# Channel tiles of an input projection in pairs, by seven products of quarters in place of eight

## Chip, core and metric

The kernel runs on one core of a Trainium2 chip. The metric is the device time of one execution in microseconds (us); the median of three runs is given where one number stands for a kernel. A profile is one further execution, recorded by the hardware.

## The reference

One layer of a hybrid model for 128 context tokens and 512 latent tokens, width 1024. The input projection `u = h @ w_in` gives all inputs of two head groups:

```python
h = _rms(x, norm_pre_w) * (1 + scale) + shift            # scale, shift, gate from c @ w_mod
u = h @ w_in                                             # 1024 -> 6176 columns
z, xbc, dt_raw, q, k, v, g = jnp.split(u, ...)
xbc = silu(_dwconv(xbc, conv_w, conv_b))                 # 3 taps along the tokens
xs, Bm, Cm = jnp.split(xbc, ...)
y_s, sf, sb = _bidir(Cm, Bm * dt, ..., xs, ...)          # chunked scans, both directions
y_s = _rms((y_s + D * xs) * silu(z), ssd_norm_w)
y_r, rf, rb = _bidir(rope(q), rope(k), ..., v, ...)      # retention, per-head decay
y_r = groupnorm(y_r) * ret_norm_w * silu(g)
out = concat([y_s, y_r]) @ w_out
y = x + gate * _rms(out, norm_post_w)
```

Outputs are `y` for both token sets and the final scan states of the context tokens. Everything is fp32.

## The kernel before

Every large product is made in three terms: each operand is split into a high part in the fp32r type and the fp32r remainder, and high x high, high x low and low x high are added up in PSUM. Activations are split once (`hh`, `hl`, 8 row tiles of 128 x 640 tokens); weights come as pieces of 256 KB (`raw`), are cast on ScalarE (`whi`, line 174) and subtracted on VectorE (`wlo`, line 175, drawn with the helper's line 131). `feed` (182) issues loads and splits some pieces ahead of their use, `take` (190) hands them out.

A start phase, written out by hand in `START` (44), normalises and modulates the activations while a first product (`gemm0`) already runs. Then the work goes by four head groups. `gemm_r` (447) makes v and g of a group by `gemm_wide` (432: five PSUM banks of 512 columns, one for each token tile, filled side by side) and q and k by `gemm_tok` (417: one token tile after the other, evicted by `ev_qk`, 384, which applies the rotation). `gemm_s` (505) makes the four channel tiles B, C and two of xs, `gemm_z` (514) two gate tiles of the group before, all by `gemm_ch` (463): channels on the partitions, 640 tokens as two halves of 320 columns, 8 row tiles x 3 terms x 2 halves = 48 matmuls a tile. `ev_conv` (478) copies the halves to `u` and does the convolution and SiLU, `ev_z` (494) the gate.

Beside these products run small steps of the scan (`s_steps`, 761) and of retention (`r_steps`, 614). They are given due times in slots: `slot` (201) is called between matmuls, feeds the weights and emits the steps that are due; an iteration over a group has 66 slots (20 in v/g, 10 in q/k, 12 in z, 24 in the channel tiles). `job` (207) spreads a list of steps over slots, lines 926 to 938. The framework then orders each engine's instructions by their place in the program, taking a later one where an earlier one is not expected to be ready; each engine's queue is in order on the chip.

Retention and scan results go to DRAM (`mixd`) and are loaded back (`load_mix`, 1003), scaled and split for the output product: `gemm_wide` three times and, for the last 512 columns, `gemm_out` (1020) in blocks of 256 columns. `ev_last` (1076) and `out_row` (1064) normalise, gate and store.

## Time and profile before

| | |
|---|---|
| median of 3 runs | 606.78 us (606.14 to 609.61) |
| profiled execution | 606.02 us, of which the span from first to last instruction is 604.0 us |
| granted TensorE clock | 0.993 of full speed over the span |
| busy share of TensorE, VectorE, ScalarE, GpSimd | 96%, 69%, 56%, 5% |
| DMA | 87.44 MB, mean 145 GB/s |

The busy share is an average over stages. TensorE's matmuls overlap and their ends are modelled, so its share isn't read as peak use; the distance from the start of one matmul to the start of the next is the better price. VectorE and ScalarE work through their queues in order.

### The profile page before, as it was taken

What the parts mean: (1) busy time and instruction counts of PE and PEld (TensorE: products, weight loads), DVE (VectorE), ACT (ScalarE), POOL (GpSimd) and SP (SyncE); (2) the same over time, 40 slices, a digit from 0 to 9 for tenths busy, and PEclk for the clock granted to TensorE, in tenths of its full rate; (3) what the DMA queues carried; (4) which work ended last, traced back from release to release, by engine and by line L of the source; (5) the groups of instructions that cost most, each with busy time, mean ns of one, the idle gap of its engine ahead of it and who ended that gap; (6) DMA issues with size and microseconds to landing.
All of it is one profiled execution on the core that took longest, in us unless ns stands there. A gap on an engine that the chain in (4) does not pass through costs nothing.

```text
span 604.0 us, 10966 instructions
## 1 busy us (share of the span) xinstructions
PE 582.3 (96%) x3833; PEld 521.5 (86%) x3833; DVE 418.1 (69%) x942; ACT 337.4 (56%) x934; POOL 31.3 (5%) x112
## 2 busy tenths in 40 slices
PE   5899998999999999999999999999999999999995
PEld 3577998978999998889999888999999777788895
DVE  3657498855698866668897746798867866743665
ACT  5436255665667764465766646566755857262421
POOL 1000001200000010000011000000110000000010
PEclk9899999999999999999999999999999999999998
DMA  8694231553335633232554223354537777384033
GB/s 348 229 362 161 63 105 48 162 146 109 99 97 159 185 91 86 80 122 70 189 172 112 76 69 105 102 163 131 160 96 223 209 266 221 116 272 120 18 109 135
DMA packets 47638, 87.44 MB, mean 145 GB/s; under 512 B 5792, under 2 KB 18656, under 8 KB 46048
## 3 DMA queue, kind: packets, MB, share of 16 engines
q1 hardware_dynamic: 47296, 86.57, 45.2%
q8 instruction: 30, 0.49, 0.3%
q14 instruction: 24, 0.20, 0.1%
q10 hardware_dynamic: 288, 0.18, 0.1%
HBM read 75.03 MB, written 9.60 MB: 140 GB/s over the span
## 4 chain that ended last, share of the span: by engine, by line
PE 65%; DVE 13%; ACT 9%; DMA 6%; issue 5%; POOL 2%; SPq 0%; POOLq 0%; DVEq 0%; ACTq 0%
PE gw L123 24%; PE gc L123 11%; PE gt L123 9%; PE acc L123 5%; PE go L123 4%; DMA cf<-cumd 3%; PE ss L123 2%; PE mod L123 2%; DVE wlo L131 2%; DVE SC L128 2%; PE sfb L123 1%; PE ry L123 1%; POOL sm L131 1%; DVE yc L128 1%; ACT jk L733 1%
## 5 line engine op out<-in xcount | busy, mean ns | idle before, releaser
L131 DVE TENSOR_TENSOR wlo<-raw,whi 128x512 fp32r<-128x512 f32 (+1 forms) x120 | 82.2, 690 | 49.2 <-ACT whi L174 48.3
L174 ACT CAST whi<-raw 128x512 fp32r<-128x512 f32 (+1 forms) x120 | 73.6, 619 | 76.3 <-PE gw L123 46.1
L123 PE MATMUL gc<-hh,whi 128*128 128x320 f32 x384 | 96.7, 331 | 0.0
L123 PE MATMUL gc<-hl,whi 128*128 128x320 f32 x384 | 88.3, 310 | 0.0
L123 PE MATMUL gc<-hh,wlo 128*128 128x320 f32 x384 | 87.6, 309 | 0.0
L123 PEld LDWEIGHTS gc<-hh,whi 128*128 128x128 f32 x384 | 63.9, 189 | 1.1
L123 PEld LDWEIGHTS gc<-hl,whi 128*128 128x128 f32 x384 | 64.3, 188 | 0.1
L123 PEld LDWEIGHTS gc<-hh,wlo 128*128 128x128 f32 x384 | 64.1, 188 | 0.0
L123 PE MATMUL gw<-whi,hh 128*128 128x512 f32 x120 | 50.6, 421 | 0.8 <-ACT u L484 0.8
L123 PE MATMUL gw<-whi,hl 128*128 128x512 f32 x120 | 47.0, 392 | 0.0
L123 PE MATMUL gw<-wlo,hh 128*128 128x512 f32 x120 | 46.8, 390 | 0.0
L123 PE MATMUL gt<-whi,hh 128*128 128x256 f32 (+1 forms) x160 | 46.3, 289 | 0.0
L123 PE MATMUL gt<-wlo,hh 128*128 128x256 f32 (+1 forms) x160 | 45.7, 286 | 0.0
L123 PE MATMUL gt<-whi,hl 128*128 128x256 f32 (+1 forms) x160 | 45.7, 286 | 0.0
L862 ACT ACTIVATE m<-gu,dt 128x128 f32<-128x128 f32 x80 | 31.3, 391 | 16.5 <-DVE gu L131 14.6
L834 ACT ACTIVATE cf<-cf,dmc 128x128 f32<-128x128 f32 x80 | 26.5, 393 | 18.4 <-DMA cf<-cumd 18.4
L131 DVE TENSOR_TENSOR m<-m,cf 128x512 f32<-128x512 f32 x40 | 27.5, 689 | 8.8 <-ACT cf L863 8.2
L123 PE MATMUL gw<-whi,mrh 128*128 128x512 f32 x80 | 32.3, 404 | 0.0
L123 PE MATMUL gw<-wlo,mrh 128*128 128x512 f32 x80 | 31.2, 391 | 0.0
L123 PEld LDWEIGHTS gt<-whi,hh 128*128 128x128 f32 x160 | 30.5, 190 | 0.7 <-issue 0.5
L863 ACT ACTIVATE cf<-gu,dt 128x128 f32<-128x128 f32 x80 | 31.0, 387 | 0.0
L123 PE MATMUL gw<-whi,mrl 128*128 128x512 f32 x80 | 30.9, 391 | 0.0
(232 smaller groups left out, 1327.8 us busy)
## 6 DMA issues: line engine op xcount, KB each, us to landing
raw<-ws SPq DMA_DIRECT2D x116, 256.0 KB, 2.8
cf<-cumd SPq DMA_DIRECT2D x20, 512.0 KB, 4.2
wm<-wm SPq DMA_DIRECT2D x8, 1024.0 KB, 8.2
mraw<-mixd SPq DMA_DIRECT2D x16, 320.0 KB, 3.4
ef<-ecumd SPq DMA_DIRECT2D x32, 128.0 KB, 3.3
wg<-wg SPq DMA_DIRECT2D x4, 1024.0 KB, 5.9
x<-x SPq DMA_DIRECT2D x5, 512.0 KB, 7.3
mixd<-rmix SPq DMA_DIRECT2D x20, 128.0 KB, 2.7
```

What stands on the lines that cost most here:

```text
L123: r = pe.matmul(out, lhsT=a, rhs=b, start=start, stop=stop)
L128: eng.scalar_tensor_tensor(out=out, in0=in0, scalar=s, in1=in1, op0=op0, op1=op1)
L131: return eng.tensor_tensor(out=out, in0=a, in1=b, op=op)
L174: act.copy(hi, raw)
L733: act.activation(jk, yc[:, h], AF.Square, scale=P ** -0.5, accum_out=sm[:, 2 + h:3 + h])
L834: act.activation(cf[:, e, 1, q], cf[:, e, 1, q], AF.Identity, bias=dmc[:, c, h:h + 1])
L862: act.activation(m[:, e, q], gu[:, 0], AF.Copy, scale=dt[:, c, h:h + 1])
L863: act.activation(cf[:, e, 1, q], gu[:, 1], AF.Copy, scale=dt[:, c, 16 + h:17 + h])
```

## The change

**Pairs.** Two channel tiles are made together by `gemm_pair`: the 1024 rows of the weights fall into two halves, the two tiles are two column halves, and the tokens fall into two halves of 322 columns (640 tokens and two zero columns behind the context tokens and two at the end, `TW`, `HW`, `off`). A 2 x 2 product of blocks is then made with seven block products in place of eight, after Winograd's form of Strassen's method. Sums of activation halves are made once (`sums`, into `sh`, `sl`); sums of weight blocks are made per pair: two of the seven pieces by a load followed by a load that adds onto it, issued by GpSimd, and two by VectorE from pieces that are there. Three PSUM banks hold the seven products in turn, and VectorE and ScalarE take them out between the products.

**Work area.** To make room for `sh` and `sl`, the scan's buffers (`sw`) and retention's (`rw`) are allocated and released in turn in one area, so the two no longer overlap in time; the due times change with that.

**Beside these.** q and k are made by `gemm_wide` too, with all five token tiles side by side; the first product takes its weights from the same stream; there are six `raw` buffers and five of `whi`, `wlo` in place of four and seven, and pieces are split four ahead; the scan's skip term is added in its own steps; the last output product uses 512 columns, and its weights are split into the place of `hh`, `hl`; the retention half of the output product's input is loaded into the memory of the right-hand area that `rp` and `tp` (`sh`, `sl`) had.

The core of the diff:

```diff
-START: ... H7:0123 G6:34 G6:012 H7:4 F2 G7:012 G7:34
+START: ... H7:0123 T0 G6:34 G6:012 T1 H7:4 F2 G7:012 T2 G7:34        # T: sums
@@ plan
+    def pair(a, b):
+        lo, hi = list(range(4)), list(range(4, 8))
+        a11, a12, a21, a22 = (("w_in", k, [(c, c + P)]) for c in (a, b) for k in (lo, hi))
+        load(*a11)
+        want.append(("sum", (-1, 2)))
+        load(*a11, a21)
+        load(*a21, a22)
+        load(*a12)
+        want.append(("sum", (-4, -1)))
+        load(*a22)
@@ load, split, feed
+            if i:
+                pool.dma_start(out=out, in_=src, accum_op=ALU.add)
+            else:
+                sp.dma_start(out=out, in_=src)
...
+    def split(n):
+        raw = pieces[n]
+        for m in (n + 1, n + 4):
+            if m < len(want) and want[m][0] == "sum" and n - m == min(want[m][1]):
+                x, y = (pieces[m + d] for d in want[m][1])
+                tt(pieces[m], x, y, ALU.add)
...
+        act.copy(hi, raw)
+        tt(lo, raw, hi.bitcast(F32), ALU.subtract)
...
+        while state["ld"] < min(len(want), state["sp"] + 6, state["use"] + 10):
+            load(state["ld"])
+            state["ld"] += 1
+        while state["sp"] < min(first, state["ld"], state["use"] + 4):
+            split(state["sp"])
+            state["sp"] += 1
@@ activations
+    def sums(k):
+        a, b, c, d = (rows[k + i][:, h * HW:(h + 1) * HW] for i in (0, 4) for h in range(2))
+        tt(d, b, d, ALU.subtract)
+        tt(b, a, b, ALU.subtract)
+        tt(a, d, a, ALU.subtract)
+        tt(c, c, a, ALU.add)
+        for i in range(2):
+            r = rows.pop(k + 4 * i)
+            q = slice(2 * i, 2 * i + 2)
+            hi, lo = (x[:, k, q].rearrange("p q t -> p (q t)") for x in (sh, sl))
+            act.copy(hi, r)
+            tt(lo, r, hi.bitcast(F32), ALU.subtract)
@@ q and k
-        gemm_tok(288 if p == 0 else 256, lambda t, ps: ev_qk(p, t, ps))
+        gemm_wide(hh, hl, lambda t, ps: ev_qk(p, t, ps), off, *((288, 1) if p == 0 else (256, 2)))
@@ channel tiles: gemm_ch, ev_conv and ev_z go
+    def gemm_pair():
+        ua, ub = (us[(turn["u"] + e) % 4] for e in range(2))
+        turn["u"] += 2
+        a0, a1, b0, b1 = (u[:, 1 + h * HW:1 + (h + 1) * HW] for u in (ua, ub) for h in range(2))
+        s1 = sp_.tile([P, HW], F32, tag="s1", name="s1", bufs=2)
+        X, Y, Z = (pg.tile([P, 512], F32, tag="g", name="gc")[:, 0:HW] for _ in range(3))
...
+        steps = [
+            (X, half(0, 0), True, lambda: act.copy(s1, X)),
+            (Y, sm(0), True, lambda: tt(b0, Y, s1, ALU.add)),
+            (Z, sm(3), True, None),
+            (Y, sm(1), False, lambda: (tt(b1, Y, s1, ALU.add), tt(b1, Z, b1, ALU.subtract))),
+            (X, half(0, 4), False, lambda: act.copy(a0, X)),
+            (Y, half(1, 4), False, lambda: tt(a1, Y, s1, ALU.add)),
+            (Z, sm(2), False, lambda: tt(b0, Z, b0, ALU.subtract)),
+        ]
+        for n, (ps, of, first, then) in enumerate(steps):
+            wh, wl = take()
+            for i in range(4):
+                xh, xl = of(i)
+                mm(ps, wh[:, i], xh, first and i == 0, False, again=True)
+                mm(ps, wh[:, i], xl, False, False, again=True)
+                mm(ps, wl[:, i], xh, False, i == 3, big=True, again=True)
+                if i == 3 and then:
+                    then()
+                if i == 3 or (i == 1 and n < 5):
+                    slot()
+        return ua, ub
@@ due times
-    job(dt_steps(), 11, 24.5)
-    job(r_steps(0), 10, 33)
+    job(dt_steps(), 10.5, 22)
+    job(r_steps(0), 12, 33)
...
-        s_job(g - 1, n + 2.5, n + 43.5, n + 51.75)
+        a, b = s_steps(g - 1)
+        job(a, n + 1, n + 36)
         gemm_r(g)
-        job(r_steps(g), n + 31.25, n + 67.25)
+        job(r_steps(g), n + 37, n + 65.5)
         gemm_z(g - 1)
+        job(b, n + 42.5, n + 43.5)
         gemm_s(g)
@@ the scan's chunk, its skip term
+                    for e in range(2):
+                        y = S[g]["xs"][e][:, off(c):off(c) + P]
+                        stt(y, y, pkc(PK_D, 2 * g + e), o[:, e])
+                if 4 in cs:
+                    sw[0].release()
@@ output product
-    ldr = load_mix(1, mrh, mrl, wp, 4)
+    ldr = load_mix(1, mrh, mrl, op)
...
+            for a, n in ((0, 512),) if t < NCK - 1 else ((0, 256), (256, 256)):
```

## Rows read from the trace of the kernel before

**Rows 1.** The page: busy time and share of each engine; the chain by engine.
```profile
PE 582.3 (96%) x3833; PEld 521.5 (86%) x3833; DVE 418.1 (69%) x942; ACT 337.4 (56%) x934; POOL 31.3 (5%) x112
...
PE 65%; DVE 13%; ACT 9%; DMA 6%; issue 5%; POOL 2%; SPq 0%; POOLq 0%; DVEq 0%; ACTq 0%
```

**Rows 2.** Windows: stretch, length, busy (x) of PE, PEld, DVE, ACT, POOL; clock; DMA.
```profile
62.60:78.60 16.00, 16.00 (x122) 16.00 (x121) 7.50 (x23) 4.47 (x14) 0.27 (x6) 1.00 0.12 32
78.60:122.40 43.80, 41.27 (x291) 39.69 (x290) 37.93 (x107) 24.91 (x82) 6.55 (x19) 1.00 0.39 115
283.50:340.00 56.50, 56.10 (x409) 54.85 (x409) 47.06 (x98) 39.41 (x120) 5.32 (x19) 1.00 0.47 141
...
230.70:340.00 109.30, 108.34 (x730) 100.84 (x729) 80.47 (x173) 67.15 (x195) 5.73 (x23) 1.00 0.39 116
```

**Rows 3.** Timeline of TensorE (start, length, instruction): columns 320, 512, 256.
```profile
305.45 0.46 PE L123 MATMUL gc<-hh,whi 128*128 128x320 f32 x2
...
306.92 0.46 PE L123 MATMUL gc<-hh,wlo 128*128 128x320 f32 x2
...
470.64 0.39 PE L123 MATMUL gw<-wlo,mrh 128*128 128x512 f32 x1
470.87 0.39 PE L123 MATMUL gw<-whi,mrh 128*128 128x512 f32 x1
...
596.81 0.28 PE L123 MATMUL go<-whi,msh 128*128 128x256 f32 x1
...
596.93 0.28 PE L123 MATMUL go<-wlo,msh 128*128 128x256 f32 x1
```

**Rows 4.** Groups of VectorE by line, whole span: busy us, mean ns, idle before.
```profile
L131 DVE TENSOR_TENSOR wlo<-raw,whi 128x512 fp32r<-128x512 f32 (+1 forms) x120 | 82.2, 690 | 49.2 <-ACT whi L174 48.3
L128 DVE SCALAR_TENSOR_TENSOR zg<-zth,gc 128x320 f32<-128x320 f32 x16 | 7.1, 483 | 1.1 <-ACT zth L498 1.1
L128 DVE SCALAR_TENSOR_TENSOR xs<-u,cw,xs 128x641 f32<-128x641 f32 x16 | 14.2, 886 | 6.5 <-ACT xs L486 6.3
L128 DVE SCALAR_TENSOR_TENSOR xs<-cth,xs 128x641 f32<-128x641 f32 x8 | 6.6, 826 | 0.7 <-ACT cth L490 0.7
```

**Rows 5.** Timeline of VectorE, two independent neighbours.
```profile
306.75 0.68 DVE L131 TENSOR_TENSOR wlo<-raw,whi 128x512 fp32r<-128x512 f32 x1
307.35 0.68 DVE L131 TENSOR_TENSOR Sst<-Sst,els 128x512 f32<-128x512 f32 x1
```

**Rows 6.** VectorE's groups in 283.5 to 340.0, and (last two) in 230.7 to 283.5.
```profile
L131 DVE TENSOR_TENSOR m<-m,cf 128x512 f32<-128x512 f32 x6 | 4.1, 689 | 0.2
L131 DVE TENSOR_TENSOR cf<-cf 128x512 f32<-128x512 f32 x3 | 2.1, 685 | 0.7 <-ACT cf L834 0.7
L128 DVE SCALAR_TENSOR_TENSOR y<-xs,pk,y 128x512 f32<-128x512 f32 x2 | 1.4, 750 | 0.0
...
L131 DVE TENSOR_TENSOR ta<-gt,rope 128x256 f32<-128x256 f32 x4 | 1.7, 423 | 1.5 <-PE gt L123 1.5
L131 DVE TENSOR_TENSOR kw<-rk,rtail 128x256 f32<-128x256 f32 x2 | 0.8, 420 | 0.0
```

**Rows 7.** A window in which VectorE is densest over 20 us.
```profile
76.62:96.62 20.00, 18.72 (x135) 18.37 (x135) 19.13 (x56) 9.99 (x28) 0.17 (x3) 1.00 0.29 83
```

**Rows 8.** The output product's first matmul (timeline), and its input's load (DMA issues, 466 to 480).
```profile
468.96 2.98 ACT L1009 ACTIVATE mrh<-mraw,nrm 128x640 fp32r<-128x640 f32 x4
...
469.84 0.50 PE L123 MATMUL gw<-whi,mrh 128*128 128x512 f32 x1
...
mraw<-mixd SPq DMA_DIRECT2D x4, 320.0 KB, 3.6
```

**Rows 9.** DMA issues (KB each, median us to landing), and a GpSimd step (timeline).
```profile
raw<-ws SPq DMA_DIRECT2D x116, 256.0 KB, 2.8
cf<-cumd SPq DMA_DIRECT2D x20, 512.0 KB, 4.2
...
304.96 0.71 POOL L131 TENSOR_TENSOR sm<-sm,mhalf 128x2 f32<-128x2 f32 x1
```

More of the change, by code (lines that the diff above doesn't have):

```diff
@@ L21 @@
 T = 640
+TW = 644
+HW = 322
 NCK = 5
@@ new lines, in plan, with sources @@
+        pair(B0 + p * P, C0 + p * P)
+        pair(XS0 + p * 256, XS0 + p * 256 + P)
+    pair(Z0 + 768, Z0 + 768 + P)
+    for half, cb in ((1, 0), (1, 2), (0, 0), (0, 2)):
+        for k in range(KT):
+            load("w_out", [8 * half + k], [(cb * 256, cb * 256 + 512)])
+    return want
+def sources():
+    at, size, order = {}, 0, []
+    for kind, of in plan():
+        for m, rows, cols in of if kind == "load" else ():
+            key = (m, tuple(rows), tuple(cols))
+            if key not in at:
+                at[key] = size
+                size += len(rows) * sum(b - a for a, b in cols)
+                order.append((m, rows, cols))
+    return at, size, order
@@ L178, in body, with load @@
[L178 to L184 removed]
+    where = sources()[0]
+    state = {"ld": 0, "sp": 0, "use": 0}
+    pieces, split_of, late = {}, {}, {}
+    def load(n):
+        kind, of = want[n]
+        nk, c = (4, P) if kind == "sum" else (len(of[0][1]), sum(b - a for a, b in of[0][2]))
+        raw = pieces[n] = wp.tile([P, nk, c], F32, tag="raw", name="raw", bufs=6)
+        for i, (m, rows, cols) in enumerate(of if kind == "load" else ()):
+            a = P * where[m, tuple(rows), tuple(cols)]
+            src = io["ws"][a:a + P * nk * c].rearrange("(p x) -> p x", p=P)
+            out = raw.rearrange("p k c -> p (k c)")
+            if i:
+                pool.dma_start(out=out, in_=src, accum_op=ALU.add)
+            else:
+                sp.dma_start(out=out, in_=src)
@@ L198, in body, with take @@
+    def take():
+        feed()
+        n = state["use"]
+        state["use"] += 1
+        pieces.pop(n)
+        return split_of.pop(n)
     jobs = []
@@ L321, in h_tile @@
         ash = ash_t[kt]
[L322 removed]
+        row = h_row(kt)
         tr = bank("tr")
```

438 lines of the change are left out of this document (201 added, 237 removed).

## Prediction

> **What bounds the kernel now.** I read the page's busy shares and its chain first, then the stages by window, then inside one stage the groups by line and the order in time. The shares name TensorE: busy 96% of the span, and 65% of the chain is its matmuls [rows 1]. VectorE, at 69%, looks as if it had room. The windows say otherwise [rows 2]: an iteration over a head group (109.3 us) has a first part, 52.8 us long, where VectorE works 33.4 us, and a second part, the channel tiles (283.5 to 340.0), where it works 47.1 of 56.5 us, 83%. In the channel tiles of group 0 it is 37.9 of 43.8 us, 87%. TensorE sets the end everywhere, but in the stages that this change rewrites VectorE is close behind. That is the thing to see before costing anything: the change takes work from TensorE and gives work to VectorE, in the same stages.
>
> **TensorE's part.** Matmuls of 320 columns start 0.147 us apart (ten of them, five rows, from 305.45 to 306.92) [rows 3], so the spacing, not the 0.31 to 0.33 us that one is drawn with, is its price. A pair of tiles costs 96 of them now, 14.1 us; after, 7 products x 4 row tiles x 3 terms = 84 of 322 columns, at 0.148 us (the spacing scaled by 322/320) 12.4 us. Saved: 1.7 us a pair, 20.4 us over 12 pairs. The last output product has 240 matmuls of 256 columns at 0.12 us (28.8 us) and gets 96 of 512 at 0.23 and 48 of 256 at 0.12 [rows 3], 27.8 us: 1.0 us less. If nothing else moved, the kernel would lose 21 us.
>
> **VectorE's part, per pair.** Seven pieces of weights are split in place of four, so three more subtractions; two pieces are sums that VectorE makes itself; five half-tile evictions (322 columns, out of PSUM) replace copies of ScalarE. One subtraction is 0.69 us, one 320-column operation that reads PSUM 0.48 us [rows 4]. Independent neighbours overlap: the one at 306.75 takes 0.68 us, and the next starts 0.60 us later [rows 5]. I therefore charge 0.60 for 512 columns and 0.40 for 322: 5 x 0.60 + 5 x 0.40 = 5.0 us a pair, 60 us in all. No row shows the sum of two pieces; the subtraction has its shape and operand count, so I take that. The z pairs replace four half-tile operations by two full ones, which is even.
>
> **The channel stage of an iteration (before: 56.5 us, VectorE 47.1).** Three pairs add 15.0. The scan now ends six slots into this stage rather than thirteen, because scan and retention take turns in one area: two of the three chunks that fall here leave (two thirds of 4.1 for m and of 2.1 for cf, and about 1.8 of their smaller steps) [rows 6], minus 5.9. The skip term (1.4) [rows 6] goes into the scan's own steps, of which one chunk stays: minus 0.9. Against that, the q/k product now finishes its five token tiles together, so three of four rotations (1.2 us each: the 0.42 and the small ones behind it [rows 6], less the overlap) slide in: plus 3.5. Retention starts after the scan, not 1.25 slots before this stage's own work: plus 2.2 for its key weighting (0.8 [rows 6]) and its decay tables. The convolutions of the last pair (each 2 x 0.80 and 0.74 after overlap [rows 4], both now after its last eviction) move out for 2.1. Sum: 47.1 + 15.0 - 5.9 - 0.9 + 3.5 + 2.2 - 2.1 = 58.9 us that VectorE must do before TensorE can leave the stage. TensorE itself needs about 56.5 - 5.1 - 2 = 49.4. So VectorE becomes the bound here. Its densest 20 us were 96% busy [rows 7]; at 95% it needs 62.0 us.
>
> How much of that can TensorE run ahead of? Pieces are split four ahead of use: 4 x 12 x 0.148 = 7.1 us of matmuls. After the last pair two of the five banks are free, so TensorE can start the next wide product on two token tiles with those four pieces, 4 x 2 x 3 x 0.23 = 5.5 us; I count half, 2.7, since the split pieces are partly the same cover. 62.0 - 7.1 - 2.7 = 52.2 us, 4.3 less than before. The ends are 49.4 (all lag covered) and 62.0 (none).
>
> The first part of the iteration loses some of this: it is full of matmuls, and two chunks of the scan move into it. I put their matmuls at 2 us (0 to 4; all small matmuls of the channel stage are 56.5 - 288 x 0.147 = 14.2), and the five banks that the q/k product now asks for at once, while ScalarE and VectorE are still emptying them, at 0.7 (0 to 2). VectorE has 38 of 55 us there, room enough. An iteration: -4.3 + 2.7 = -1.6 us; three: -4.8.
>
> **The other stages.** Group 0's channel tiles: 37.9 + 10.0 + 3.5 - 2.1 = 49.3 us, at 95% 51.9, less 9.8 of cover: 42.1 against 43.8, -1.7 (38 to 52). The activation sums: four calls, each four half-row operations (0.40) and two row subtractions (0.74), 12.5 us of VectorE, most of which fits into the 8.5 us that it idles in the first q/k product [rows 2]; three calls stand ahead of the last activation tile, so some of it delays TensorE: +1 (0 to 4). The z pair of group 3: -1.7, but the retention half of the output product now loads its input into memory that the sums hold until that pair's last matmul. Before, its first matmul came at 469.84, right behind the conversions; now the load (3.6 us) comes first [rows 8]. Scan matmuls fill part of the hole: +1.7 (0 to 3.6). The extra ScalarE casts and the dropped copies about cancel; ScalarE has 39.4 of 56.5 us [rows 2]. The stores and the last row's chain keep their length.
>
> **Sum**, against the profiled 606.0 us: -4.8 - 1.7 + 1 + 0 - 1.0 = -6.5, 599.5. The median of the runs is 0.8 above the profiled execution; I predict 600.5.
>
> **Rivals.**
> First, *the whole gain* (0.17). If the planned order lets TensorE work far enough ahead, the lag is covered everywhere: 606.8 - 21 + 2 = 588. For it: over the kernel VectorE would have 418 + 60 + 12 = 490 of 586 us, 84%. Against it: it is short in just the stages where nothing can be put off, since a product that reuses a bank two steps later (1.8 us a step) waits for VectorE to empty it.
>
> Second, *no cover* (0.21). Evictions are queued behind whatever VectorE has ready, and the second use of a bank comes two steps on. If that slack is all there is, each channel stage takes 62.0, i.e. 9.8 more than forecast: 600.5 + 3 x 9.8 less what the convolutions behind it give back (about 2 each) = 624; with half of it, 612. It decides from the point where VectorE's backlog passes two steps, 3.5 us.
>
> Third, *the adding transfers* (0.17), which end slower. Two pieces of a pair arrive by a load and a second transfer that adds onto it, issued by GpSimd once the first has landed. The first sum needs the piece three places on, whose buffer is free only three pieces earlier, 3 x 12 x 0.148 = 5.3 us. A load lands in 2.8 us, one of twice the bytes in 4.2 [rows 9]. No row shows an adding transfer: it takes 2.8 if it is like a load, 4.2 if reading its destination counts as bytes; its issue is no shorter than a small GpSimd operation's 0.71 [rows 9], or it is nothing. So 5.6 to 7.7 us; I take 6.3 (2.8 + 0.7 + 2.8), 1.0 more than the lead. VectorE's queue is in order, so a sum that waits holds evictions, convolutions and retention behind it; and GpSimd's queue, waiting for the load, holds retention's variance step, on which VectorE already waits. In the forecast the split lead hides it; without that it is 12 pairs x 1.0 = 12 us: 612 (up to 12 x 2.4 = 29).
> The Trainium skill, "SBUF — State Buffer", section "SBUF: two separate sides", has a rule that speaks against this part of the change: the descriptors of a DMA issued by GpSimd are written by GpSimd itself, and it cannot write them while VectorE runs a copy in a two-port mode; it gives 3.1 us for a transfer that takes 0.62 alone. By that figure the estimate would be 24 x 2.5 = 60 us, if a copy lay on each transfer. The long VectorE rows of the channel stage are two-input operations, not copies, so I give this no chance of its own beyond the third rival's.
>
> Last, *the order of the columns* (0.05): if 322 columns, or rows that start two columns off, stream slower than the 320 of now, 1008 x 0.015 = 15 us of the gain goes: 615.
>
> **How the numbers follow.** The forecast, 594 to 607, has 0.40. Faster by over 0.5% (about what a measurement of this kernel can tell from no change) means under 603.7: 0.30 of the forecast's 0.40 and the first rival's 0.17, 0.47. Slower means over 609.8: two thirds of the second and third rivals and the last, with a little of the rest, 0.32. Within: 0.21. The range reaches down to 588 and up to 619, leaving out the far ends of the second and third rivals. The likeliest case's own range is 594 to 607.
>
> **What would show it.** Right: in the channel windows VectorE at 93% or more, TensorE's idle time before channel matmuls ended by evictions or split pieces, the stage at 50 to 55 us, the first part of an iteration 1 to 4 us longer, 322-column matmuls 0.148 us apart. The first rival: TensorE dense throughout and the stage at 47 to 50. The second: the stage at 58 or more, with VectorE saturated. The third: VectorE idle ended by an adding DMA, or GpSimd's variance step late. I would be wrong altogether if VectorE's operations on sums or evictions cost other than their shape's row, or if the stage before the first channel tile grew by more than 4 us.

## The result

The changed kernel takes 639.9 us (636.9 to 642.2, four runs), the kernel before 606.8 in the same comparison: a ratio of 1.053, 95% interval 1.048 to 1.059. That is 33 us slower, where 600.5 was forecast with a range up to 619. The profiled execution took 638.6 us, its span 636.6. Of the four runs of e15 below, one was slow (627.3 us) and is left out of its time and ratio.

By stage, each up to the last matmul of the product named (the two parts of the output product meet at the first matmul of the second), in the two profiled executions (us):

| stage | before | after |
|---|---|---|
| start, to the last accumulation of the first product | 62.7 | 65.4 |
| first q/k product and channel tiles of group 0 | 58.8 | 68.6 |
| iteration 1 | 109.3 | 114.7 |
| iteration 2 | 109.2 | 115.8 |
| iteration 3 and the last z pair | 128.3 | 132.4 |
| to the first matmul of the output product | 1.5 | 4.6 |
| output product, wide part | 98.9 | 99.6 |
| last output product and end | 35.3 | 35.5 |

Every stage has grown; the last line, where 1.0 us of gain was forecast, by 0.2.

### The profile page after: what moved, and what is told of

Its sections match the earlier page's. It is cut to its first block, busy times and chain, and to the rows that moved or that the text cites. A ratio compares the mean times of both kernels' runs of the same rounds, so it can differ in the third digit from the quotient of the medians.

```text
span 636.6 us, 10789 instructions
## 1 busy us (share of the span) xinstructions
PE 583.9 (92%) x3593; PEld 506.1 (79%) x3593; DVE 483.1 (76%) x1091; ACT 357.1 (56%) x942; POOL 54.8 (9%) x112
## 4 chain that ended last, share of the span: by engine, by line
PE 54%; DVE 16%; DMA 11%; ACT 11%; issue 5%; SPq 1%; POOL 1%; DVEq 0%; POOLq 0%; ACTq 0%
PE gw L154 20%; PE gc L154 14%; DMA cf<-cumd 6%; PE acc L154 4%; PE go L154 3%; DVE wlo L162 2%; PE ry L154 2%; PE mod L154 2%; ACT cf L923 2%; DMA ef<-ecumd 2%; ACT cf L952 2%; ACT m L951 1%; DVE SC L159 1%; DMA raw<-ws 1%; PE rs L154 1%
## 5 line engine op out<-in xcount | busy, mean ns | idle before, releaser
L154 PE MATMUL gw<-whi,hh 128*128 128x512 f32 (+2 forms) x280 | 97.2, 355 | 5.6 <-DVE rzg L159 5.1
L154 PE MATMUL gw<-wlo,hh 128*128 128x512 f32 (+2 forms) x280 | 93.8, 336 | 0.0
L154 PE MATMUL gw<-whi,hl 128*128 128x512 f32 (+2 forms) x280 | 93.2, 335 | 0.0
L154 PE MATMUL gc<-sh,whi 128*128 128x322 f32 x192 | 66.2, 345 | 8.8 <-DVE u L162 8.6
L154 PEld LDWEIGHTS gw<-whi,hh 128*128 128x128 f32 x280 | 52.9, 192 | 12.5 <-DVE rzg L159 5.9
L154 PE MATMUL gc<-sl,whi 128*128 128x322 f32 x192 | 62.4, 325 | 0.0
L154 PE MATMUL gc<-sh,wlo 128*128 128x322 f32 x192 | 61.8, 322 | 0.0
L154 PEld LDWEIGHTS gw<-whi,hl 128*128 128x128 f32 x280 | 53.5, 191 | 5.0
L154 PEld LDWEIGHTS gw<-wlo,hh 128*128 128x128 f32 x280 | 53.6, 192 | 4.3
L154 PE MATMUL gc<-hh,wlo 128*128 128x322 f32 x144 | 47.6, 330 | 0.8 <-DVE wlo L162 0.8
```

Source lines behind the costliest of these rows:

```text
L154: r = pe.matmul(out, lhsT=a, rhs=b, start=start, stop=stop, skip_group_check=again)
```

## The profile after

The page: busy time by engine, the chain by engine, and the loads of weight pieces by SyncE and by GpSimd (KB each, median us from issue to landing).

```profile
PE 583.9 (92%) x3593; PEld 506.1 (79%) x3593; DVE 483.1 (76%) x1091; ACT 357.1 (56%) x942; POOL 54.8 (9%) x112
...
PE 54%; DVE 16%; DMA 11%; ACT 11%; issue 5%; SPq 1%; POOL 1%; DVEq 0%; POOLq 0%; ACTq 0%
...
raw<-ws SPq DMA_DIRECT2D x136, 256.0 KB, 3.0
...
raw<-ws POOLq DMA_DIRECT2D x24, 256.0 KB, 4.5
```

Against [rows 1], TensorE's share of the chain fell from 65% to 54%, and VectorE, DMA and ScalarE hold what it gave up. VectorE works 483 us, against 418 before; the forecast's addition gave 490.

Windows (stretch, length, busy time and count of PE, PEld, DVE, ACT, POOL, granted clock, DMA share, GB/s): the first q/k product, the channel tiles of group 0, then iteration 2 in its first part, its channel stage and whole.

```profile
65.40:83.50 18.10, 16.28 (x121) 15.77 (x119) 11.11 (x27) 8.84 (x26) 2.31 (x10) 1.00 0.48 126
83.50:134.00 50.50, 44.22 (x270) 40.48 (x270) 46.41 (x132) 24.18 (x77) 6.75 (x12) 0.93 0.40 106
...
248.70:305.80 57.10, 52.98 (x329) 46.30 (x328) 38.87 (x75) 37.20 (x106) 2.75 (x4) 0.97 0.46 132
305.80:364.50 58.70, 55.42 (x369) 52.22 (x367) 54.93 (x132) 34.30 (x91) 8.28 (x13) 0.97 0.50 129
...
248.70:364.50 115.80, 108.40 (x695) 98.52 (x693) 93.80 (x206) 71.50 (x197) 11.04 (x16) 0.97 0.48 130
```

Against [rows 2], the channel stage of an iteration has grown from 56.5 to 58.7 us although it has 252 channel matmuls in place of 288, and its first part, where VectorE has 18 us to spare, from 52.8 to 57.1. Adding up every channel matmul's time from its own start to the next matmul's start gives 183.8 us after (1008 of them) and 183.7 before (1152). The saving of 20 us is there in the spacing, whose median is 0.149 us, and all of it is lost again between them, in waits and in stretches at half clock (last section). The q/k matmuls of groups 1 to 3 grew from 44.0 to 51.4 us by the same addition, and the small matmuls of scan and retention by about 16.

TensorE's waits over the span (engine, line, what it waited for: us in total, times, longest), after:

```profile
PE gc L154 <- DVE u L162: 8.6, 3, 3.1
PE gw L154 <- DVE rzg L159: 5.1, 3, 2.7
PE mod L154 <- DVE silc L354: 5.0, 1, 5.0
PE st L868 <- ACT tok L869: 4.1, 3, 1.5
PE cums L154 <- DVE s L162: 3.1, 1, 3.1
PE gw L154 <- ACT mrh L1100: 3.1, 1, 3.1
```

The same view of before, its three longest:

```profile
PE mod L123 <- DVE silc L266: 4.8, 1, 4.8
PE tr L325 <- DVE x L279: 2.1, 2, 1.5
PE ry L123 <- DVE rm L131: 1.3, 1, 1.3
```

Two of the new waits show how they arise. The first is an eviction that stands in VectorE's queue. Timeline of VectorE (start, length, instruction) in the channel stage of iteration 2:

```profile
331.32 0.82 DVE L162 TENSOR_TENSOR xs<-xs,u 128x644 f32<-128x644 f32 x1
332.18 0.42 DVE L817 TENSOR_REDUCE sm<-ry 128x2 f32<-128x256 f32 x1
332.52 0.82 DVE L162 TENSOR_TENSOR xs<-xs,u 128x644 f32<-128x644 f32 x1
333.25 0.82 DVE L162 TENSOR_TENSOR sqacc<-sqacc,u 128x644 f32<-128x644 f32 x1
333.99 0.41 DVE L159 SCALAR_TENSOR_TENSOR yc<-sm,ry 128x256 f32<-128x256 f32 x1
334.39 0.83 DVE L162 TENSOR_TENSOR sqacc<-sqacc,u 128x644 f32<-128x644 f32 x1
335.13 0.68 DVE L162 TENSOR_TENSOR wlo<-raw,whi 128x512 fp32r<-128x512 f32 x1
335.74 0.49 DVE L162 TENSOR_TENSOR u<-gc,s 128x322 f32<-128x322 f32 x1
336.14 0.41 DVE L162 TENSOR_TENSOR rm<-rg,Dr 128x256 f32<-128x256 f32 x1
```

TensorE at the same place, with its idle time and what ended it in brackets:

```profile
332.75 0.31 PE L154 MATMUL gc<-hl,whi 128*128 128x322 f32 x1
332.89 0.31 PE L154 MATMUL gc<-hh,wlo 128*128 128x322 f32 x1
336.28 0.63 PE L154 MATMUL gc<-sh,whi 128*128 128x322 f32 x1 [3.08 <-DVE u L162]
336.71 0.47 PE L154 MATMUL gc<-sl,whi 128*128 128x322 f32 x1
336.98 0.47 PE L154 MATMUL gc<-sh,wlo 128*128 128x322 f32 x1
```

The final steps of the scan (`xs`, `sqacc`) and one weight piece are ahead of `u<-gc,s`, which empties the bank that the next product wants. VectorE does not idle here; it does other work first.

The second is the change to the q/k product in the same iteration. ScalarE, VectorE and TensorE:

```profile
281.99 0.39 ACT L460 ACTIVATE th<-gw 128x256 f32<-128x256 f32 x1
285.18 0.40 ACT L923 ACTIVATE cf<-cf,dmc 128x128 f32<-128x128 f32 x1 [2.80 <-DMA cf<-cumd]
285.49 0.35 ACT L456 COPY rv<-gw 128x256 f32<-128x256 f32 x1
...
286.29 0.39 ACT L460 ACTIVATE th<-gw 128x256 f32<-128x256 f32 x1
```

```profile
282.41 0.42 DVE L159 SCALAR_TENSOR_TENSOR rzg<-th,gw 128x256 f32<-128x256 f32 x1
286.72 0.42 DVE L159 SCALAR_TENSOR_TENSOR rzg<-th,gw 128x256 f32<-128x256 f32 x1 [3.88 <-ACT th L460]
```

```profile
284.21 0.28 PE L154 MATMUL gw<-whi,hl 128*128 128x256 f32 x1
287.19 0.39 PE L154 MATMUL gw<-whi,hh 128*128 128x256 f32 x1 [2.70 <-DVE rzg L159]
```

Here VectorE idles 3.9 us. ScalarE waits 2.8 us for the scan's decay load (`cf<-cumd`), the evictions of the v/g product stand behind that in its queue, VectorE's `rzg` waits for ScalarE, and TensorE, which has done two of the five token tiles of q/k, waits for the third bank. Before, the q/k product finished tile by tile and needed one bank at a time.

## The experiments

All ratios are to the kernel before, run beside each, with 95% intervals. The kernel before took 606.8 to 608.8 us in these comparisons, and most intervals reach 2 to 4 us to either side, so a difference between two versions is good to some 3 to 5 us. In the diffs a line of "..." marks what is left out.

| run | what it is | us | ratio |
|---|---|---|---|
| after | the change | 639.9 | 1.053 [1.048, 1.059] |
| e1 | adding transfers made plain loads | 628.4 | 1.037 [1.030, 1.043] |
| e2 | 25.6 us of VectorE's work left out | 641.3 | 1.055 [1.049, 1.061] |
| e3 | final scan steps later | 637.5 | 1.049 [1.045, 1.053] |
| e4 | before, with the changed due times | 608.3 | 0.999 [0.997, 1.001] |
| e5 | eight products, rest as changed | 624.6 | 1.029 [1.023, 1.035] |
| e6 | q/k by token tiles, five buffers | 639.1 | 1.052 [1.048, 1.055] |
| e7 | a bank for each product | 631.2 | 1.040 [1.035, 1.044] |
| e8 | all seven pieces plain | 629.0 | 1.036 [1.030, 1.042] |
| e9 | e5, q/k by token tiles, seven buffers | 613.6 | 1.010 [1.006, 1.014] |
| e10 | e5, own storage for y and z | 624.7 | 1.026 [1.020, 1.033] |
| e11 | e5, own area for retention | 618.5 | 1.018 [1.010, 1.026] |
| e12 | e7 and e8 together | 612.9 | 1.008 [1.004, 1.012] |
| e13 | e5, seven buffers alone | 620.2 | 1.020 [1.014, 1.027] |
| e14 | e12 with the room of e9 and e11, no sums | 601.2 | 0.990 [0.986, 0.994] |
| e15 | the changed pair with the room of e9 and e11 | 617.0 | 1.016 [1.012, 1.019] |
| e16 | own banks, sums on GpSimd, all computed | 641.1 | 1.053 [1.050, 1.057] |
| e17 | before, wide last output product | 607.6 | 0.999 [0.997, 1.002] |
| e18 | e9 and e11 together | 613.4 | 1.009 [1.006, 1.013] |

### Is VectorE the bound, or its queue, or the transfers?

The theory on record was a channel stage in which VectorE has more to do than TensorE. Four runs set it against its rivals.

e1, the two adding transfers of a pair:

```diff
-        load(*a11, a21)
-        load(*a21, a22)
+        load(*a21)
+        load(*a22)
```

> The two adding transfers of each pair are left out: those two pieces are loaded plainly (so the products of the channel tiles are not the reference's); VectorE's, ScalarE's and TensorE's work stays as it is. Theory of the queue (in the channel stages VectorE is the bound, and what TensorE waits for stands behind other VectorE work): 634 to 640 us, no more than 5 below the changed kernel, because no engine that is late loses work. Theory of the adding transfers (late pieces hold VectorE's and GpSimd's queues): at least 12 pairs x 1 us less, 628 or under.

Measured 628.4, 11.5 us less than the change, or 10 by the two ratios, since the kernel before was 2 us slower beside e1. The adding transfers cost that, close to the third rival's price (12).

e2, two of the three taps of each convolution:

```diff
-        stt(out, u[:, 0:TW], cw[:, ct:ct + 1], out)
-        stt(out, u[:, 2:TW + 2], cw[:, 32 + ct:33 + ct], out)
```

> The two side taps of the convolution are left out, two VectorE operations of 644 columns (0.80 us each after overlap) a channel tile, 25.6 us of VectorE in 16 tiles, and nothing of TensorE's; everything else as in the changed kernel. Theory of the queue: each channel stage gets shorter by most of the 6.4 us that VectorE loses there, so 614 to 624. Theory of the adding transfers, or of a chain of dependences in which the taps do not stand: 632 or more.

Measured 641.3, no gain at all. The channel stage of iteration 1, of the changed kernel and of e2, and TensorE's longest waits in e2:

```profile
189.90:248.70 58.80, 55.45 (x369) 52.06 (x367) 54.72 (x133) 34.34 (x93) 8.04 (x13) 0.97 0.49 128
```

```profile
190.80:247.50 56.70, 53.22 (x358) 50.42 (x357) 50.40 (x126) 33.40 (x89) 8.19 (x13) 0.97 0.51 128
```

```profile
PE gc L154 <- DVE u L162: 8.6, 3, 3.1
PE sy L154 <- DVE m L162: 6.0, 6, 1.6
```

VectorE does 4.3 us less in this stage, the stage is 2.1 shorter, and the part in front of it (57.6 in place of 55.9) takes most of that back. The evictions wait 8.6 us as before, because what stands ahead of them is the scan's final steps, not the taps. With all else as changed, VectorE's sum of work is not the bound; what stands ahead of an eviction at one moment is. The run cannot say what that sum would cost once the other waits are gone.

e3, the scan's final steps later:

```diff
-        job(b, n + 42.5, n + 43.5)
+        job(b, n + 46, n + 53)
```

> The changed kernel with the scan's last two steps (gate, square, sum: about 3.3 us of VectorE in one piece) due at slots 46 to 53 of an iteration, not at 42.5 to 43.5, where they stand right ahead of the first evictions of the B/C pair. Theory of the queue with short slack (TensorE can wait out little more than two steps of a pair, and after a wait of 3 us its clock is at half for 3.4 us): the wait of about 3 us and the slow stretch behind it go in three iterations, 624 to 632. Theory of throughput alone (VectorE's total in the stage decides, the order doesn't): 636 to 641.

Measured 637.5, an interval that overlaps the change's. The 3.1 us waits for `u` are gone, and the time turns up at other places:

```profile
PE gw L154 <- DVE rzg L159: 6.5, 3, 3.3
...
PE sy L154 <- DVE m L162: 4.8, 4, 2.0
...
PE rz L834 <- DVE yc L159: 3.7, 6, 0.8
```

So the most visible wait was not a cause by itself. The time lies in the range that was set for "throughput alone", but e2 speaks against that theory; what fits both is that another wait takes the place of the one removed.

e4, the other way round: the kernel before with scan and retention taking turns in time, but not in memory.

```diff
-        s_job(g - 1, n + 2.5, n + 43.5, n + 51.75)
+        a, b = s_steps(g - 1)
+        job(a, n + 1, n + 36)
...
-        job(r_steps(g), n + 31.25, n + 67.25)
+        job(r_steps(g), n + 37, n + 65.5)
```

> The kernel before with the due times of the changed kernel: scan and retention no longer overlap, nothing else is changed. Theory of the queue: 603 to 612, since VectorE gets no work and the channel tiles of this kernel have long slack. Theory of the turns (that running scan and retention one after the other costs the time by itself, through their chains): 617 or more.

Measured 608.3, the same time as before. The order in time costs nothing where the rest is as it was.

### The pair, or the room made for it?

The sums of the activations need memory (`sh`, `sl`), and most of the other edits exist to free it. e5 takes the pair away and leaves the room as changed:

```diff
-        X, Y, Z = (pg.tile([P, 512], F32, tag="g", name="gc")[:, 0:HW] for _ in range(3))
...
+        for u in out:
+            ps = [pg.tile([P, 512], F32, tag="g", name="gc")[:, 0:HW] for _ in range(2)]
+            for k in range(KT):
...
+            for h in range(2):
+                act.copy(u[:, 1 + h * HW:1 + (h + 1) * HW], ps[h])
...
-T0 G6:34 G6:012 T1 H7:4 F2 G7:012 T2 G7:34
+G6:34 G6:012 H7:4 F2 G7:012 G7:34
```

> The changed kernel with the channel tiles computed by eight products again (96 matmuls of 322 columns a pair, eight quarter pieces loaded plainly, halves evicted by ScalarE, no sums of activations or weights); the shared area, the due times and the q/k product over five banks stay as changed. If the pair product itself (its evictions, its sums, its pieces) is what costs, the time returns to that of the kernel before, give or take the 1 us of the output product: 604 to 611. If the shared area and the five banks of q/k are the cause, it stays at 625 to 640, since the eight products add 20 us of TensorE and take nothing of those two away.

Measured 624.6, just under the second range. Of the 33 us, the room, with the edits that came beside it, costs 17 and the pair 15 on top of it, though the pair takes 20 us of matmuls away. So half of the loss has nothing to do with the seven products.

e6, the q/k product alone, in the changed kernel (`gemm_tok` as in the kernel before, with four pieces held and one split ahead):

```diff
-        gemm_wide(hh, hl, lambda t, ps: ev_qk(p, t, ps), off, *((288, 1) if p == 0 else (256, 2)))
+        if p:
+            gemm_tok(256, lambda t, ps: ev_qk(p, t, ps))
+        else:
+            gemm_wide(hh, hl, lambda t, ps: ev_qk(p, t, ps), off, 288)
```

> The changed kernel with the q/k product of groups 1 to 3 finished token tile by token tile, as before the change, instead of five tiles at once; all else as changed (while it runs, only one further piece is split ahead). The q/k matmuls cost 7.4 us more in the changed kernel than before, and the waits on the gating step in front of them 5.7. If the five banks asked for at once are a cause of their own, 626 to 633. If they only show a lateness that arises elsewhere, 636 to 643.

Measured 639.1: nothing. It did not tell the theories apart, since four of the five buffers of split pieces are held while it runs, so that the channel tiles behind it begin with one piece in place of four: TensorE's waits for a cast before a channel matmul rose from nothing to 4.7 us. By the addition from start to start, its q/k matmuls of groups 1 to 3 came back from 51.4 to 43.6 us, and its channel matmuls rose from 183.8 to 193.9.

e7, no bank used twice in a pair:

```diff
-        X, Y, Z = (pg.tile([P, 512], F32, tag="g", name="gc")[:, 0:HW] for _ in range(3))
...
+            ps = pg.tile([P, 512], F32, tag="g", name="gc")[:, 0:HW]
+            bk.append(ps)
```

> The changed kernel with each of a pair's seven products in a bank of its own, in turn over the five, so a bank comes back five steps later and not two; this leaves out the additions across products that share a bank, so the channel tiles are not sums of all their parts. Same matmuls, same evictions, same pieces. If the reuse two steps on is what exposes TensorE to late evictions (10 us of waits on evicted halves and some of the half-speed stretches behind them), 622 to 630. If the lateness comes from a chain elsewhere, the wait only moves and it stays at 636 to 643.

Measured 631.2: 8.7 us less, 1 us above the first range. Its channel stages of iterations 1 and 2:

```profile
187.30:239.40 52.10, 51.35 (x355) 48.74 (x354) 50.53 (x123) 31.85 (x85) 7.03 (x11) 1.00 0.50 128
303.60:356.30 52.70, 50.88 (x355) 48.75 (x355) 50.98 (x124) 31.90 (x85) 7.28 (x11) 1.00 0.48 125
```

They took 58.8 and 58.7 us in the changed kernel. VectorE's sum over the kernel is about the same (480 us for 483), and some 4 us of it have moved out of each channel stage. A part of the gain is lost elsewhere: the first part of iteration 2 takes 64.2 us in place of 57.1.

e8, plain pieces without any sum of weights:

```diff
-        load(*a11)
...
+        for w in (a11, a12, a21, a22, a12, a11, a22):
+            load(*w)
```

> The changed kernel with all seven pieces of a pair loaded plainly: no adding transfer and no VectorE sum of two pieces, so the products take pieces that are not the quarter sums (the channel tiles come out other than the reference's). Leaving out the adding transfers alone gave 628. If the pieces' chain (load, adding transfer, sum on VectorE that waits for pieces three places on) is the main cause, 605 to 618. If VectorE's in-order queue of evictions is, the 14 us less on VectorE are worth little, 624 to 629.

Measured 629.0, the same as e1 within the intervals. VectorE's 24 sums, 14 us of work, cost nothing that shows; the adding transfers do.

### What the room costs

Four versions with eight products, in which the memory of the sums is free and one edit each is undone.

e9, the edit of e6 with three pieces split ahead, and with the buffers for it:

```diff
-            hi = wp.tile(list(raw.shape), F32R, tag="whi", name="whi", bufs=5)
-            lo = wp.tile(list(raw.shape), F32R, tag="wlo", name="wlo", bufs=5)
+            hi = wp.tile(list(raw.shape), F32R, tag="whi", name="whi", bufs=7)
+            lo = wp.tile(list(raw.shape), F32R, tag="wlo", name="wlo", bufs=7)
```

> The version with eight products a pair and everything else as changed took 624.6, 17 us over the kernel before, so the room that was made for the sums costs by itself. Here its q/k product of groups 1 to 3 is finished token tile by token tile again, with seven buffers of split pieces in place of five (the memory of the sums is free). If the five banks at once and the thin stock of pieces are that cost, 609 to 616; if not, 621 to 627.

Measured 613.6: 11 of the 17 us.

e10, own tiles for the scan's output, the gated z and its square:

```diff
-            stt(z, th, 1.0, z, ALU.add, ALU.mult)
+            zg = sp_.tile([P, TW], F32, tag=f"zg{e}", name="zg")
+            stt(zg, th, 1.0, z, ALU.add, ALU.mult)
...
-                        stt(y, y, pkc(PK_D, 2 * g + e), o[:, e])
+                        stt(L["y"][e][:, q], S[g]["xs"][e][:, q], pkc(PK_D, 2 * g + e), o[:, e])
```

> The version with eight products a pair, with storage of its own for the scan's output, the gated z and its square, in place of working in the convolutions' and the channel tiles' own tiles. In the changed kernel a channel tile's eviction waits 3.2 us behind the final steps of the scan that hold its storage. If this reuse is the cost of the room, 609 to 616; if not, 621 to 627.

Measured 624.7: nothing.

e11, retention in memory of its own:

```diff
-            rw[0] = tc.alloc_tile_pool(name="rw", bufs=1, side="left")
+            rw[0] = tc.alloc_tile_pool(name="rw", bufs=1, side="right" if p else "left")
```

> The version with eight products a pair, with an area of its own for retention of groups 1 to 3, on the other side of the memory; the turns in the due times stay (which cost 1.5 us or nothing in the kernel before). If scan and retention wait for each other's release of the shared area (loads of state that hold SyncE's queue and with it the weight loads, tables that wait for the last scan step), 609 to 616; if not, 621 to 627.

Measured 618.5, between the two expectations: 6 us less, though its interval overlaps that of e5.

e13, e9's buffers without its q/k product:

```diff
...
-            lo = wp.tile(list(raw.shape), F32R, tag="wlo", name="wlo", bufs=5)
...
+            lo = wp.tile(list(raw.shape), F32R, tag="wlo", name="wlo", bufs=7)
```

> The version with eight products a pair (624.6), with seven buffers of split pieces in place of five and the q/k product over five banks as changed. Together with the q/k product by token tiles this gave 613.6. If the thin stock of split pieces was what cost there (ScalarE's casts stand in its queue until TensorE gives a buffer back), 612 to 617. If the five banks asked for at once were, 621 to 627.

Measured 620.2, between the two: some 4 us of e9's 11 may be the two buffers and some 7 the five banks. The first part is not shown, since the interval overlaps that of e5; the second rests on intervals that just miss each other.

e18, e9 and e11 in one kernel, that is, to e9:

```diff
-            rw[0] = tc.alloc_tile_pool(name="rw", bufs=1, side="left")
+            rw[0] = tc.alloc_tile_pool(name="rw", bufs=1, side="right" if p else "left")
```

> Eight products a pair, q/k of groups 1 to 3 by token tiles, seven buffers of split pieces and retention's own area: the whole room given back, the pair as before. If q/k with its buffers (11 us) and the area (6) are the room's whole price, 606 to 610, the kernel before. The version with seven products and the same room took 601.2, so the pair's 20 us of matmuls would then be worth 5 to 9 of them even with its additions, its adding transfers and its reuse of banks left out. If the two overlap, 611 to 615.

Measured 613.4, as e9 alone. The area's 6 us do not come on top of what e9 gave back. A reading that fits, but that no run shows, is that with one bank wanted at a time a step that comes late from the shared area no longer stops TensorE. Of the room's 17 us, 5 to 6 are left (ratio 1.009, from 1.006) that no run here assigns; in its profiled execution (616.0, the longest of its four) they are spread over the start (65.1), the iterations (110.6, 111.4, 130.4) and the output product (100.5).

### Do the causes add up?

e12, e7 and e8 in one kernel, that is, to e8:

```diff
-        X, Y, Z = (pg.tile([P, 512], F32, tag="g", name="gc")[:, 0:HW] for _ in range(3))
...
+            ps = pg.tile([P, 512], F32, tag="g", name="gc")[:, 0:HW]
+            bk.append(ps)
```

> The changed kernel with both: all seven pieces loaded plainly without sums, and a bank for each product; the channel tiles are then not the reference's, and the additions across products are left out. Each alone gave 629.0 and 631.2 against 639.9. If the two act on different waits, 618 to 623. If both only relieve the same late VectorE queue, 625 to 630. 605, the eight-product version less 20 us of matmuls, would mean that nothing else of the pair costs anything.

Measured 612.9, below the ranges of both theories and 27 us less than the change, where the two alone gave 8.7 and 10.9. The 7 us beyond their sum are just clear of the intervals. Each hides the other: with the pieces plain, TensorE still waits 5.3 us for late evictions of channel halves (e8), and with free banks 5.0 us for late pieces (e7); here the two together come to under 3.

e15, the room alone given back to the changed pair (the products of the sums read the quarters themselves):

```diff
-            return lambda i: (sh[:, i, q], sl[:, i, q])
+            return lambda i: (hh[:, 2 * i + q // 2, q % 2 * HW:(q % 2 + 1) * HW], hl[:, 2 * i + q // 2, q % 2 * HW:(q % 2 + 1) * HW])
```

> The changed pair as it is (adding transfers, sums of weights, two banks' reuse), without the sums of the activations (their products read the quarters themselves, so the channel tiles are not the reference's), and with the memory so freed the q/k product of groups 1 to 3 by token tiles, seven buffers and retention's own area. If the room that the sums take is half of the loss and independent of the pair, 639.9 less 19: 618 to 624. If the pair's own waits take the place of what is freed, 630 to 640.

Measured 617.0: where the pair stays, the room, with the sums, is some 23 of the 33 us.

e14, all of it; to e15:

```diff
-        load(*a11, a21)
-        load(*a21, a22)
...
+        for w in (a11, a12, a21, a22, a12, a11, a22):
+            load(*w)
...
+            ps = pg.tile([P, 512], F32, tag="g", name="gc")[:, 0:HW]
+            bk.append(ps)
```

> Seven products with every price named so far taken away: all pieces loaded plainly, a bank for each product, no sums of the activations (their products read the quarters themselves; with the plain pieces and the missing additions the channel tiles are not the reference's), and with the memory so freed the q/k product of groups 1 to 3 by token tiles, seven buffers of split pieces and an area of its own for retention. If the causes add up, 612.9 less 11 for q/k and buffers, 6 for the area and 2 for the sums: 594, which is the kernel before less most of the 21 us of matmuls. If something of the pair is still unnamed, 602 to 610.

Measured 601.2, the only version with seven products below the kernel before; it leaves out the sums and the additions without which the seven products are not the channel tiles. Its iterations 1 and 2:

```profile
122.00:229.50 107.50, 104.76 (x695) 95.88 (x693) 93.08 (x210) 73.92 (x207) 8.41 (x12) 1.00 0.55 169
229.50:334.20 104.70, 104.28 (x694) 95.96 (x692) 88.26 (x198) 70.65 (x197) 7.50 (x10) 1.00 0.47 140
```

TensorE is busy 97 and 99.6% of them, at full clock. Against e18, which has the same room, the pair is worth 12.2 us of its 20.4 when its additions and its adding transfers are left out. What takes the other 8 was not settled.

### Can it be mended, and is a part worth keeping?

e16 computes all of it, with a bank for each product (the additions across products made at eviction) and with the second part of a piece loaded plainly and added by GpSimd:

```diff
-                pool.dma_start(out=out, in_=src, accum_op=ALU.add)
+                add = sp_.tile([P, nk, c], F32, tag="add", name="add", bufs=1)
+                sp.dma_start(out=add.rearrange("p k c -> p (k c)"), in_=src)
+                tt(raw, raw, add, ALU.add, eng=pool)
```

> The changed kernel computing all of it, with two mends: a bank for each of the seven products, the additions across products made at eviction (two more VectorE operations a pair), and the adding transfers replaced by a plain load into one more buffer and an addition on GpSimd. If the two prices are the pair's own, most of what the version with plain pieces and own banks gained (27 us) comes back: 616 to 624. If GpSimd's additions are late or hold VectorE, 628 to 640. It is not expected under 607, since the shared memory and the q/k product stay.

Measured 641.1: no mend. The waits for evicted channel halves are gone from TensorE's list, and one for split pieces heads it:

```profile
PE gc L154 <- DVE wlo L162: 16.2, 14, 3.6
```

An addition on GpSimd took 1.37 us (24 of them, 33.0 us in all), and there is one buffer for what it adds. The trace shows one cost more. Two equal steps of VectorE, the second beside such an addition:

```profile
327.58 0.82 DVE L162 TENSOR_TENSOR xs<-xs,u 128x644 f32<-128x644 f32 x1
328.63 1.28 POOL L162 TENSOR_TENSOR raw<-raw,add 128x512 f32<-128x512 f32 x1 [3.50 <-DMA raw<-ws]
328.78 1.81 DVE L162 TENSOR_TENSOR xs<-xs,u 128x644 f32<-128x644 f32 x1
```

Added up, the operations of VectorE that overlap the 24 additions take 15 us longer than the medians of the same operations elsewhere in the run. Which of the three, the addition's length, the one buffer or VectorE's slower steps, makes the pieces late, no run separates.

e17, the last output product alone, put into the kernel before:

```diff
-            for n, cb in enumerate(cbs):
...
+            for a, n in ((0, 512),) if t < NCK - 1 else ((0, 256), (256, 256)):
```

> The kernel before with one part of the change alone: the last output product in matmuls of 512 columns (the last token tile in two of 256), its pieces of one row tile by 512 columns and its last rows as changed. The matmuls of that product took 22.2 + 5.6 us in the changed kernel against 28.4 before, so 0.6 us less: 605.5 to 607.0. If the last row's chain, which the wider evictions lengthen by 0.4 to 0.8 us, takes it back: 606.5 to 608.

Measured 607.6 beside 608.6, ratio 0.999 [0.997, 1.002]: no difference that this measurement shows. No version run here that computes all of it is clearly faster than the kernel before.

## Why the prediction was wrong

**The matmuls and VectorE's prices were right.** 322 columns cost 0.149 us (forecast 0.148); an eviction's place in VectorE's queue is 0.40 us (the next operation after 335.74 starts at 336.14) and a piece's 0.61 (335.13 to 335.74), as charged; VectorE's whole is 483 (forecast 490), and 54.9 us in the channel stage of iteration 2 (forecast 58.9).

**The step that failed is the cover in the channel stage:** "62.0 - 7.1 - 2.7 = 52.2 us", VectorE's demand less 9.8 us by which TensorE was to run ahead. The stage takes 58.8 and 58.7 us in iterations 1 and 2, so only some 3 of the 9.8 were there. The cover was counted from split pieces and free banks after the last pair, and not from the banks inside a pair, where the second use comes two steps on. With a bank for each product (e7) the stage takes 52.1 and 52.7 us, the forecast's own number, with VectorE 97% busy in it.

This is one half of the second rival, which asked for a stage of 58 or more with VectorE saturated. Its other half, that VectorE's sum of work sets the stage, is not borne out: VectorE is 94% busy there, but e2 leaves out 25.6 us of its work and takes the same time, and so does e8 against e1 with 14 us. What delays TensorE is the order in which the in-order queues of VectorE and ScalarE come to the one operation that frees a bank or delivers a piece: in one example VectorE is busy with other things, in the other it idles behind ScalarE behind a load.

**A second term was put at next to nothing: the room.** The sum has 0.7 us an iteration for it, the five banks; with eight products it costs 17 us (e5). Of that, five buffers of split pieces in place of seven may be some 4 us (e13, an interval that overlaps e5's a little).

**Five banks at once** had a term, 0.7 us an iteration (0 to 2). Runs e13 and e9 put it at some 2.2 (6.6 us over three), just above its bound, and only with the pieces in stock. The first part of an iteration came out at 55.9, 57.1 and 54.5 us, against 55.5 forecast.

**The shared area** was costed as turns in time: work moved between stages. In time they cost nothing (e4). In memory they cost about 6 us where q/k wants five banks and the stock is thin (e11, intervals that overlap), and nothing that shows otherwise (e18). No step of the prediction had that.

**The adding transfers**, the third rival, were sized well and left out of the sum. Forecast 12 us if the split lead did not hide them; they cost 10 to 11.5 (e1). The chain is longer than the 6.3 us assumed: from the load's issue to the landing of what is added, the 24 pieces took 7.3 to 10.4 us, 8.4 in the median (the load 3.0, some 0.6 to the issue of the second transfer, and 4.5 from there to landing, with the 0.91 of the issue in it). The signs set for this rival showed little: VectorE idles for an adding transfer once, 5.5 us in front of the first pair's sum, and its waits for retention's variance step fell from 18.5 to 2.8 us. So the price is shown, and the way by which it reaches TensorE is not. The row for the issue, from the groups of GpSimd over the span:

```profile
L204 POOL DMA_DIRECT2D raw<-ws x24 | 21.3, 909 | 257.5 <-DMA raw<-ws 81.3 <-DVE xw L162 54.5 <-ACT u L602 43.1
```

The rule that was set beside it then (the Trainium skill, "SBUF — State Buffer", section "SBUF: two separate sides") would have put it at 60 us if a copy of VectorE's lay on each transfer. Each of the 24 issues took 0.86 to 1.23 us and the whole costs 10 to 11.5, so no such lock on each transfer shows here; whether it lengthens some of them no run tells.

**The reuse of banks** stood in the second rival as its slack ("the second use of a bank comes two steps on"); by itself it costs 8.7 us (e7).

**Rivals were weighed as if only one could hold.** The second (624) and the third (12 more) together make 636. That this is close to what happened is in part luck, since neither has the room in it. e12 shows that the reuse and the transfers do more than add: 27 us for both, 20 for the sum of each. The range, built from one case at a time, ended at 619.

**Group 0's channel tiles** (42.1 forecast, 38 to 52) took 50.5, inside the bounds at the far end. **The sums in the start** (+1, 0 to 4): the stage grew by 2.7, but it took 62.6 to 66.7 us in the versions that leave the sums out (e11 and e5 at the ends), so the growth is not shown to be theirs. **The handover** to the output product (+1.7, 0 to 3.6): 3.1, the load in front of the first matmul as described. **The last output product** (-1.0): its matmuls gave 0.6, the comparison nothing (e17). (Two small sums of the prediction are off: the four calls make 12.3 us, not 12.5, and 599.5 + 0.8 is 600.3, not 600.5. Nothing hangs on them.)

Of the 33 us, then: with eight products the room costs 17, of which 11 are the q/k product over five banks with the thin stock of pieces; the pair costs 15 more, where it should have given 20. Taken away together, the adding transfers (with the sums of weights) and the reuse of banks give back 27, the room after that another 12. What takes the last 8 of the 20, and the 5 to 6 of the room that are left in e18, stays open.

## What to carry to other kernels

Before giving an engine more work, look at what stands ahead of each operation that releases a buffer, in every in-order queue that it passes, and not at the engine's share: here 25 us of work could be removed without any effect, while a bank for each product gave 8.7 with the same operations. Cost the room as carefully as the change: make a version with the room and without the gain first, for it tells in one run whether the gain is worth having. And add rivals up, since waits that hide each other also come together.

## What the runs showed of the hardware

**TensorE's clock after a wait.** Windows of the changed kernel around the eviction wait shown above; the granted clock stands behind POOL's count.

```profile
332.50:336.30 3.80, 0.72 (x6) 0.46 (x4) 3.80 (x8) 2.30 (x7) 1.65 (x3) 1.00 0.98 263
336.30:339.70 3.40, 3.40 (x15) 3.38 (x15) 1.95 (x6) 0.00 (x0) 0.40 (x1) 0.50 0.78 154
339.70:343.00 3.30, 3.30 (x24) 3.20 (x24) 3.30 (x9) 2.75 (x10) 0.58 (x2) 1.00 0.17 53
```

After this wait of 3.1 us the clock is granted at half, 1.2 GHz, for 3.4 us. Two 322-column matmuls start 0.27 us apart in it (336.71 and 336.98, in the rows of TensorE above) and 0.14 to 0.15 before the wait, so 3.4 us at half cost up to 1.5 us more (an estimate from this spacing). Between the end of its first product and the end of its last the changed kernel has six such stretches, 23.9 us in all, each at the end of a wait of 1.8 to 3.2 us or within 1.4 us of it; the kernel before has none, nor has e14. By the same estimate that is up to some 10 of the 33 us, which a sum over waits does not show. Not every such wait ends so: the one of 3.1 us in front of the output product is followed by full clock (1.00 over the next 99.7 us). The Trainium skill says in "TensorE: Matmul & The Clock Gate", section "HAM oscillation — how this bites in real kernels", that matmuls which follow a wait for their data start at the slower clock again. These rows agree, for a wait on a bank; the wait in front of the output product does not.

**An adding transfer.** 256 KB added onto a tile by a transfer that GpSimd issues took 4.5 us from issue to landing, 0.91 of it the issue; a plain load by SyncE took 3.0 in the same kernel.

**VectorE beside an addition on GpSimd.** A two-input step of 128x644 took 1.81 us beside one, 0.82 otherwise (rows of e16 above).
